# The opening and the first three staged blocks of a decoder trunk, written as one pipeline with every engine's order fixed

## The chip, the cores and the metric

The kernel runs on one core of one Trainium2 chip. A core has a matrix engine (TensorE, "PE" in the profile, whose weight loads have a row of their own, "PEld"), VectorE ("DVE"), ScalarE ("ACT"), GpSimd ("POOL"), a queue engine ("SP") and 16 DMA engines, which all queues share. The metric is device time in microseconds, the median of several executions.

## The reference

A two-layer causal decoder trunk on 256 tokens of width 2048, all in float32. Every sub-layer is modulated by vectors worked out from a conditioning vector `c`:

```python
cond = silu(c)
for l in range(2):
    sh1, sc1, g1, sh2, sc2, g2 = split(cond @ ada_w[l] + ada_b[l], 6)   # ada_w[l]: 2048 x 12288
    h = rmsnorm(x, norm_mix_g[l]) * (1 + sc1) + sh1
    y = mixer_ab(h, ...) if l == 0 else mixer_c(h, ...)
    x = x + g1 * y
    h = rmsnorm(x, norm_ffn_g[l]) * (1 + sc2) + sh2
    x = x + g2 * ((silu(h @ w1) * (h @ w3)) @ w2)
return rmsnorm(x, final_g)
```

`mixer_ab` begins with one projection `h @ ab_w_in` (2048 x 4096). Its first half becomes a gated causal convolution of width 31, its second half a chunked causal gate with a layer norm and a 128 x 128 spatial weight per head. The part of the kernel that the change touches is everything from the first load to the first three 512-wide column groups of that projection.

## The kernel before, in words

The 256 tokens are two blocks `b` of 128 on the partitions. A weight is read in loads of 512 KB (`load`, L182: 256 rows by 512 columns; `load_wide`, L191: 128 rows by 1024 columns), all issued on SP and all into one ring of 12 buffers (`RAW`). For products in nearly float32 precision each load is split (L163) into a rounded `hi`, cast by ACT (L167), and a rest `lo`, subtracted by DVE (L168). The activations are split in the same way (`ah`, `al`). Each pair of 128 x 128 tiles then takes three matmuls: hi by ah, hi by al (L216, L217) and lo by ah (L222). The load's buffer is free again after the DVE subtraction. A `unit` (L198) is two loads, two splits and 24 matmuls for one quarter (512 rows) of the inner dimension and one group of 512 output columns.

The modulation vectors come from `mod_cols` (L368), a generator that works out 512 of the 2048 columns of one vector in four steps, each with two loads of `ada_w`. A scale runs on PE with the conditioning vector as the weights (L381), into a PSUM bank `ps_ada` of which there is one. A shift, except in the first quarter, runs on DVE as a weighted sum `accq` (L386, L388). At the end `put_cols` (L403) turns the row into columns: eight small PE instructions (L408) into the one-bank pool `msp`, then additions on DVE (L414, or L417 and L418).

`norm_cols` (L436) makes such a pair of generators, scale and shift, for each quarter of the inner dimension. `started` (L539) uses them in a staged way: the projection's quarter `q` can run as soon as quarter `q` of scale and shift is known. Block `q` first scales the normalised, transposed tokens (`scaled`, L492; h on ACT and DVE at L500 and L502, then the splits at L489 and L490), then runs three units, the third into two banks named `mt`. Between the halves of its units (`between`, L531) it advances the two generators of quarter `q + 1`, so that a block holds 6 weight loads and 16 adaLN loads, the last one only 6.

Before these blocks comes an opening: `consts` (L70) loads `c`, gathers six small tables by DMAs on ACT's queue into one tile `stage`, transposes it (L113), and does the same for the adaLN bias `st_b` (L121 to L124). `run` (L967) loads `x`, and takes its sums of squares on ACT (`sumsq`, L454). `mixer_ab` (L605) issues four larger tables on ACT's queue: the spatial weights (`b_w_s`, 512 KB), the convolution weights (`a_conv_w`, 31 rows, 124 KB) and two norm vectors. `entry` work (`start`, `prep`) normalises the tokens and transposes them (L477, L480, L518). `params` (L627) transposes the spatial and the convolution weights through `msp` (L636, L637, L641, L642) and spreads the two norm vectors over the partitions (`to_bcast`, L423: L432 to L434). It is called after block 0.

The order of the instructions on each engine is not that of the text. A planner sorts each engine's instructions ahead of time by priority, which is the place in the text, and by when it expects operands and buffers to be there; it may bring a later instruction forward. On the chip each engine then runs its list strictly in order. Tiles with the same tag share a fixed number of slots. The tag "t" has three, for `cs`, `stage`, `st_b`, the normalised rows `xr`, and `rhi` and `rlo` of `to_bcast`.

## Time and profile before

| | us |
|---|---|
| median of 3 runs | 2014.65 |
| lowest and highest | 2011.18 and 2015.0 |
| the profiled execution, its own time | 2018.89 |
| its span | 2017.2 |
| PE busy within the span | 1957.5 |
| DVE busy | 1420.8 |
| ACT busy | 840.2 |
| mean HBM traffic | 267 GB/s |

The profile is one execution. Its page gives each engine's busy time, the chain of work that ended last, the costliest groups of instructions (line of the code, engine, operation, result <- operands, shape, count, busy us, mean ns of one, idle time before them and what ended it), and the DMA issues. The trace behind it can be asked for stretches of time: a row then has the busy time of PE, PEld, DVE, ACT and POOL with counts, the granted clock of PE as a share of full speed, the busy share of the DMA engines and GB/s. In the order of time, a row has start, duration, engine, line, and in brackets the idle time before it with what ended that. "SPq" is the issue of a DMA by SP, not its transfer.

### The profile page before, as it was taken

The page shows a single profiled execution, that of the slowest core. Times are in us where ns is not written, and L with a number is a line of the kernel's source. Part 1 is how long each engine was busy: PE and PEld are TensorE (multiplying, and loading weights), DVE is VectorE, ACT ScalarE, POOL GpSimd, SP SyncE. Part 2 cuts the span into 40 slices and gives each one's busy share as a digit, 9 for nine tenths or more (in the row PEclk, how much of TensorE's full clock was granted, in tenths as well). Part 3 has the DMA queues.
Part 4 walks back from the last instruction along what each step waited for, and adds up shares of the span by engine and source line. Part 5 has one row for each costly group of instructions (what it writes and reads, how often), then busy time and mean ns, then how long its engine had stood idle before and what let it go on. Part 6 is the DMA issues. An engine that isn't in the chain of part 4 may idle for free.

```text
span 2017.2 us, 24298 instructions
## 1 busy us (share of the span) xinstructions
PE 1957.5 (97%) x8896; PEld 1542.4 (76%) x8896; DVE 1420.8 (70%) x1709; ACT 840.2 (42%) x1023; POOL 34.2 (2%) x91
## 2 busy tenths in 40 slices
PE   5989999998999999999999999999999999999998
PEld 2567677777887888887878887788788888888886
DVE  2667999788778888777887788867555444554455
ACT  3234343454444334443344347544433444334443
POOL 0000000000000000000120000000000000000000
PEclk9889999989999999999999999999999999999999
DMA  9998988879888899888988887889656666566651
GB/s 329 351 369 266 339 277 284 270 252 343 294 277 327 316 341 331 300 295 316 343 308 292 289 286 264 324 276 326 198 187 191 189 189 191 183 189 190 193 184 48
DMA packets 250344, 540.39 MB, mean 268 GB/s; under 512 B 16521, under 2 KB 17849, under 8 KB 249840
## 3 DMA queue, kind: packets, MB, share of 16 engines
q1 hardware_dynamic: 248472, 536.99, 78.2%
q10 hardware_dynamic: 1752, 1.86, 0.3%
q8 instruction: 69, 1.13, 0.2%
q14 instruction: 51, 0.42, 0.1%
HBM read 536.68 MB, written 2.10 MB: 267 GB/s over the span
## 4 chain that ended last, share of the span: by engine, by line
PE 95%; DVE 2%; DMA 2%; ACT 1%; issue 0%; POOL 0%; ACTq 0%; POOLq 0%; DVEq 0%
PE mm L216 28%; PE mm L217 27%; PE mm L222 27%; PE ps_ada L381 3%; PE ps_col L408 2%; PE mt L216 1%; PE mt L217 1%; PE tp L591 1%; PE mt L222 1%; DVE accq L388 1%; PE ps_ada L315 1%; PE tp L480 1%; DMA st_b<-in_ada_b_dram 1%; PE tp L838 1%; DMA raw<-in_pool_w_dram 0%
## 5 line engine op out<-in xcount | busy, mean ns | idle before, releaser
L167 ACT CAST hi<-raw 128x1024 fp32r<-128x1024 f32 x632 | 665.1, 1053 | 986.1 <-PE mm L217 898.2
L168 DVE TENSOR_TENSOR lo<-raw,hi 128x1024 fp32r<-128x1024 f32 x632 | 771.1, 1223 | 423.6 <-ACT hi L167 413.3
L216 PE MATMUL mm<-hi,ah 128*128 128x512 f32 x1568 | 619.5, 396 | 6.0 <-ACT hi L167 3.4
L217 PE MATMUL mm<-hi,al 128*128 128x512 f32 x1568 | 613.6, 392 | 0.0
L222 PE MATMUL mm<-lo,ah 128*128 128x512 f32 x1568 | 422.9, 390 | 0.0
L216 PEld LDWEIGHTS mm<-hi,ah 128*128 128x128 f32 x1568 | 296.0, 189 | 94.3 <-ACT hi L167 14.4
L217 PEld LDWEIGHTS mm<-hi,al 128*128 128x128 f32 x1568 | 296.1, 189 | 62.9 <-DVE accq L388 1.7
L222 PEld LDWEIGHTS mm<-lo,ah 128*128 128x128 f32 x1568 | 295.6, 189 | 61.7
L216 PE MATMUL mm<-hi,hh 128*128 128x512 f32 x704 | 279.9, 398 | 0.0
L217 PE MATMUL mm<-hi,hl 128*128 128x512 f32 x704 | 277.4, 394 | 0.0
L353 DVE SCALAR_TENSOR_TENSOR acc<-raw,cond,acc 128x1024 f32<-128x1024 f32 x180 | 230.6, 1281 | 5.3 <-DMA raw<-in_ada_w_dram 3.7
L222 PE MATMUL mm<-lo,hh 128*128 128x512 f32 x704 | 194.7, 395 | 0.0
L216 PEld LDWEIGHTS mm<-hi,hh 128*128 128x128 f32 x704 | 132.1, 188 | 34.7 <-ACT hi L167 1.7
L222 PEld LDWEIGHTS mm<-lo,hh 128*128 128x128 f32 x704 | 132.1, 188 | 32.1
L217 PEld LDWEIGHTS mm<-hi,hl 128*128 128x128 f32 x704 | 132.1, 188 | 30.8
L388 DVE SCALAR_TENSOR_TENSOR accq<-raw,cond,accq 128x512 f32<-128x512 f32 x135 | 101.1, 749 | 4.8 <-DMA raw<-in_ada_w_dram 2.1
L676 DVE SCALAR_TENSOR_TENSOR co<-aT,cw,co 128x256 f32<-128x256 f32 x240 | 99.5, 479 | 0.0
L216 PE MATMUL mm<-hi,mh 128*128 128x512 f32 x160 | 64.8, 406 | 1.6 <-ACT mh L489 1.6
L599 DVE TENSOR_TENSOR gy<-mm,gate 128x512 f32<-128x512 f32 x72 | 47.1, 686 | 24.3 <-PE mm L222 23.9
L217 PE MATMUL mm<-hi,ml 128*128 128x512 f32 x160 | 63.8, 401 | 0.3 <-DVE ml L490 0.3
L381 PE MATMUL ps_ada<-raw,cond 128*32 128x512 f32 x352 | 62.3, 629 | 0.0
L600 DVE TENSOR_TENSOR x<-x,gy 128x512 f32<-128x512 f32 x72 | 47.2, 688 | 0.1
(169 smaller groups left out, 990.6 us busy)
## 6 DMA issues: line engine op xcount, KB each, us to landing
raw<-in_ffn_w_dram SPq DMA_DIRECT2D x528, 512.0 KB, 4.8
raw<-in_ada_w_dram SPq DMA_DIRECT2D x384, 512.0 KB, 5.7
raw<-in_ab_w_in_dram SPq DMA_DIRECT2D x64, 512.0 KB, 6.5
raw<-in_ab_w_out_dram SPq DMA_DIRECT2D x32, 512.0 KB, 5.7
raw<-in_pool_w_dram SPq DMA_DIRECT2D x8, 512.0 KB
x<-in_x_dram SPq DMA_DIRECT2D x2, 1024.0 KB, 6.5
gate<-in_final_g_dram SPq DMA_DIRECT2D x1, 1024.0 KB
out_dram<-x SPq DMA_DIRECT2D x2, 512.0 KB
```

The source lines that it names most:

```text
L167: nc.scalar.copy(hi, raw)
L168: nc.vector.tensor_tensor(lo, raw, hi.bitcast(F32), op=ALU.subtract)
L216: nc.tensor.matmul(ps[b], act[b][0][:, kk, :], hi[:, k, :], start=first and kk == 0, stop=False)
L217: nc.tensor.matmul(ps[b], act[b][1][:, kk, :], hi[:, k, :], start=False, stop=False)
L222: self.nc.tensor.matmul(ps[b], act[b][0][:, kk, :], lo[:, k, :], start=False, stop=last and kk == 3)
L353: nc.vector.scalar_tensor_tensor(acc, raw, self.cond[:, k : k + 1], acc, op0=ALU.mult, op1=ALU.add)
L381: nc.tensor.matmul(acc[32 * j : 32 * j + 32, :], self.cond[:, k : k + 1].to_broadcast([P, 32]), raws[j // 2][:, j % 2, :], start=u == 0, s ...
L388: nc.vector.scalar_tensor_tensor(acc, raws[j // 2][:, j % 2, :], self.cond[:, k : k + 1], acc, op0=ALU.mult, op1=ALU.add)
L408: nc.tensor.matmul(ps[:, a : a + 1], src[:, P * a : P * a + P], one, start=u == 0, stop=u == len(parts) - 1,)
L599: nc.vector.tensor_tensor(t, ps, g[:, 512 * q : 512 * q + 512], op=ALU.mult)
L600: nc.vector.tensor_tensor(xs, xs, t, op=ALU.add)
L676: nc.vector.scalar_tensor_tensor(co[:, k, :], src, cw[:, k, j : j + 1], co[:, k, :], op0=ALU.mult, op1=ALU.add,)
```

## The change

The opening moves out of `consts` and `run` into a new function `opening`, whose text is a pipeline: steps of the first quarter's scale (`next(sc)`) and shift (`next(sh)`) stand between the loads of `x`, the small tables and the entry work of the two token blocks. All the small loads go on SP's queue instead of ACT's, `stage` gets a place of its own and its memset goes to POOL. The four larger tables become a function `tables`, also on SP, called after block 0; `params` is called after block 1 instead of block 0.

In `started` both loads of a unit are split before its products, and the generators advance after each half. With `staged=True` a generator of quarters 1 to 3 yields after its fourth step and not before `put_cols`, so the row copy and the column products come in the middle of the third unit. A new context manager `in_order` ties each instruction on PE, DVE, ACT and SP that is traced within it to the one before it on the same engine, which adds no wait on the chip but takes from the planner the freedom to reorder. It is put around the opening and the four blocks of the first layer's projection. `started` is also used by the first layer's channel mixer, there without the fixed order.

```diff
...
 AF = mybir.ActivationFunctionType
 ALU = mybir.AluOpType
 PSUM = bass.MemoryType.PSUM
+ENG = mybir.EngineType
+ORDERED = (ENG.PE, ENG.DVE, ENG.Activation, ENG.SP)
+AFTER = mybir.DependencyInfo(mybir.DependencyClass.NoSync, mybir.DependencyReason.DATA)
 
 P = 128
 D = 2048
...
     def consts(self):
         nc, c = self.nc, self.cpool
         i = self.i
-        cs = self.wk.tile([KT, P], F32, name="cs", tag="t", bufs=3)
-        nc.sync.dma_start(out=cs, in_=i["c"].rearrange("a (k p) -> (a k) p", p=P))
         warm = c.tile([P, 1], F32, name="warm")
         nc.vector.memset(warm, 0.0)
         nc.scalar.activation(warm, warm, AF.Silu)
...
         for j in range(4):
             nc.gpsimd.memset(self.pick[32 * j : 32 * j + 1, :], 1.0)
 
+    def opening(self, e):
+
+        nc, c, i = self.nc, self.cpool, self.i
+        sc, sh = e.parts[0]
+        cs = self.wk.tile([KT, P], F32, name="cs", tag="t", bufs=3)
+        nc.sync.dma_start(out=cs, in_=i["c"].rearrange("a (k p) -> (a k) p", p=P))
         ps = self.msp.tile([P, 512], F32, name="ps_c", tag="ms")
         nc.tensor.transpose(ps[:, :KT], cs, self.ident[:KT, :KT])
         self.cond = c.tile([P, KT], F32, name="cond")
         nc.scalar.activation(self.cond, ps[:, :KT], AF.Silu)
-        stage = self.wk.tile([P, P], F32, name="stage", tag="t", bufs=3)
-        nc.vector.memset(stage, 0.0)
+
+        def tokens(b):
+            nc.sync.dma_start(out=self.x[b], in_=i["x"][0, b * P : (b + 1) * P, :])
+            for q in range(4):
+                self.sumsq(b, q)
+
+        def entry(b):
+            e.start(b)
+            for q in range(4):
+                e.prep(b, q)
+
+        stage = c.tile([P, P], F32, name="stage")
+        nc.gpsimd.memset(stage, 0.0)
         rows = {}
         r = 0
 
         def put(name, ap, n):
             nonlocal r
-            nc.scalar.dma_start(out=stage[r : r + n, :], in_=ap)
+            nc.sync.dma_start(out=stage[r : r + n, :], in_=ap)
             rows[name] = r
             r += n
 
+        next(sc)
+        next(sc)
+        tokens(0)
+        next(sc)
         put("mix_g", i["norm_mix_g"].rearrange("l (k p) -> (l k) p", p=P), 2 * KT)
+        tokens(1)
+        entry(0)
+        next(sc)
         put("ffn_g", i["norm_ffn_g"].rearrange("l (k p) -> (l k) p", p=P), 2 * KT)
+        st = [self.wk.tile([P, P], F32, name=f"st_b{l}", tag="t", bufs=3) for l in range(2)]
+        for l in range(2):
+            nc.sync.dma_start(out=st[l][: 6 * KT, :], in_=i["ada_b"][l].rearrange("(k p) -> k p", p=P))
+        next(sh)
         put("conv_b", i["a_conv_b"].rearrange("l (k p) -> (l k) p", p=P), HT)
         put("a_g", i["a_norm_g"].rearrange("l (k p) -> (l k) p", p=P), HT)
         put("a_b", i["a_norm_b"].rearrange("l (k p) -> (l k) p", p=P), HT)
         put("b_bias", i["b_bias"].rearrange("l h t -> (l h) t"), HT)
+        next(sh)
+        self.adab = c.tile([P, 2, 6 * KT], F32, name="adab")
+        for l in range(2):
+            ps = self.msp.tile([P, 512], F32, name="ps_b", tag="ms")
+            nc.tensor.transpose(ps[:, : 6 * KT], st[l][: 6 * KT, :], self.ident[: 6 * KT, : 6 * KT])
+            nc.vector.tensor_copy(self.adab[:, l, :], ps[:, : 6 * KT])
+        entry(1)
         ps = self.msp.tile([P, 512], F32, name="ps_c", tag="ms")
         nc.tensor.transpose(ps[:, :P], stage, self.ident)
         cols = c.tile([P, P], F32, name="cols")
         nc.vector.tensor_copy(cols, ps[:, :P])
         self.col = lambda name, k: cols[:, rows[name] + k : rows[name] + k + 1]
         self.cols = lambda name, k, n: cols[:, rows[name] + k : rows[name] + k + n]
-        self.adab = c.tile([P, 2, 6 * KT], F32, name="adab")
-        for l in range(2):
-            st = self.wk.tile([P, P], F32, name="st_b", tag="t", bufs=3)
-            nc.scalar.dma_start(out=st[: 6 * KT, :], in_=i["ada_b"][l].rearrange("(k p) -> k p", p=P))
-            ps = self.msp.tile([P, 512], F32, name="ps_b", tag="ms")
-            nc.tensor.transpose(ps[:, : 6 * KT], st[: 6 * KT, :], self.ident[: 6 * KT, : 6 * KT])
-            nc.vector.tensor_copy(self.adab[:, l, :], ps[:, : 6 * KT])
+        self.close(sc)
+        next(sh)
+        next(sh)
+        self.close(sh)
 
     def bands(self, tiles):
 
...
             self.put_cols([(acc, self.ones[:, :1])], HT, l, v, HT * hh, dst, gname)
             yield
 
-    def mod_cols(self, l, v, q, on_pe, dst, gname=None):
+    def mod_cols(self, l, v, q, on_pe, dst, gname=None, staged=False):
 
 
         nc = self.nc
...
                     nc.vector.scalar_tensor_tensor(
                         acc, raws[j // 2][:, j % 2, :], self.cond[:, k : k + 1], acc, op0=ALU.mult, op1=ALU.add
                     )
-            if u < 3:
+            if u < 3 or staged:
                 yield
         if on_pe:
             rows = self.wk.tile([P, 512], F32, name="rows", tag="rows", bufs=1)
...
             parts = [(rows, self.pick)]
         else:
             parts = [(acc, self.ones[:, :1])]
-        yield
+        if not staged:
+            yield
         self.put_cols(parts, 4, l, v, 4 * q, dst, gname)
         yield
 
...
     def norm_cols(self, e, l, sc, sh, gname):
 
         e.parts = [
-            self.add(self.mod_cols(l, sc, q, True, e.gs, gname), self.mod_cols(l, sh, q, q == 0, e.sh))
+            self.add(
+                self.mod_cols(l, sc, q, True, e.gs, gname, staged=q > 0),
+                self.mod_cols(l, sh, q, q == 0, e.sh, staged=q > 0),
+            )
             for q in range(4)
         ]
 
...
             elif slot == 4:
                 self.close(g)
 
-    def started(self, e, w_cols, rate, then=None):
+    @contextmanager
+    def in_order(self):
+
+        traced = self.nc.cur_bb.bb.instructions
+        n = len(traced)
+        yield
+        before = {}
+        for ins in traced[n:]:
+            if ins.engine in ORDERED:
+                if ins.engine in before:
+                    self.tc.add_manual_dep(ins, before[ins.engine].name, AFTER, reason="in_order")
+                before[ins.engine] = ins
+
+    def started(self, e, w_cols, rate, then={}):
 
 
 
...
             e.act[q] = [self.scaled(e.act[q][b], q, b, e.gs, e.sh) for b in range(NB)]
             nxt = e.parts[q + 1] if q < 3 else ()
             for u, (w, col0) in enumerate(w_cols):
-                self.unit(
-                    w, 512 * q, col0, e.act[q], ps[u], q == 0, q == 3, lambda: self.between(nxt, 2 * u)
-                )
-                self.between(nxt, 2 * u + 1)
-            if q == 0 and then is not None:
-                then()
+                raws = [self.load(w, 512 * q + 256 * h, col0) for h in range(2)]
+                cuts = [self.split(raw) for raw in raws]
+                for h, (hi, lo) in enumerate(cuts):
+                    for b in range(NB):
+                        self.products(hi, lo, h, e.act[q], b, ps[u], q == 0)
+                    for b in range(NB):
+                        self.products_lo(hi, lo, h, e.act[q], b, ps[u], q == 3)
+                    self.between(nxt, 2 * u + h)
+                self.after_unit()
+            if q in then:
+                then[q]()
         self.rate = rate
         return ps
 
...
             cwr = raw[:, 2:, :].rearrange("p a n -> p (a n)")
             nrm = p.tile([P, 2, 512], F32, name="nrm", tag="co")
             nc.gpsimd.memset(nrm, 0.0)
-            nc.scalar.dma_start(out=ws, in_=i["b_w_s"][0].rearrange("h t s -> t h s"))
-            nc.scalar.dma_start(out=cwr[:CW, :], in_=i["a_conv_w"][0])
-            for n, name in enumerate(("b_norm_g", "b_norm_b")):
-                nc.scalar.dma_start(out=nrm[0:64:32, n, :], in_=i[name][0].rearrange("(j n) -> j n", n=512))
+
+            def tables():
+                nc.sync.dma_start(out=ws, in_=i["b_w_s"][0].rearrange("h t s -> t h s"))
+                nc.sync.dma_start(out=cwr[:CW, :], in_=i["a_conv_w"][0])
+                for n, name in enumerate(("b_norm_g", "b_norm_b")):
+                    nc.sync.dma_start(out=nrm[0:64:32, n, :], in_=i[name][0].rearrange("(j n) -> j n", n=512))
 
             def params():
 
...
                 self.to_bcast(nrm[:, 0, :], bg, 2)
                 self.to_bcast(nrm[:, 1, :], bb, 2)
 
-            for b in range(NB):
-                e.start(b)
-                for q in range(4):
-                    e.prep(b, q)
-            held = self.started(e, [(w_in, 0), (w_in, DH), (w_in, 512)], RATES[0], params)
+            with self.in_order():
+                self.opening(e)
+                held = self.started(
+                    e, [(w_in, 0), (w_in, DH), (w_in, 512)], RATES[0], {0: tables, 1: params}
+                )
             act = e.act
 
             co = p.tile([P, HT, T], F32, name="co", tag="co")
...
         nc, i = self.nc, self.i
         self.ss = [None] * NB
         self.consts()
-        self.x = []
-        for b in range(NB):
-            xb = self.xpool.tile([P, D], F32, name=f"x{b}")
-            nc.sync.dma_start(out=xb, in_=i["x"][0, b * P : (b + 1) * P, :])
-            self.x.append(xb)
-            for q in range(4):
-                self.sumsq(b, q)
+        self.x = [self.xpool.tile([P, D], F32, name=f"x{b}") for b in range(NB)]
 
         def cols(name):
             return self.cpool.tile([P, KT], F32, name=name)
...
         last = Entry(self, None, None, None)
 
         self.norm_cols(mix0, 0, SC1, SH1, "mix_g")
-        self.finish(mix0.parts[0][:1])
         self.g1 = self.gate()
         self.gen_g1 = self.add(self.bcast(0, G1, True, self.g1))
         scale = [self.mod_cols(0, SC2, q, True, ffn0.gs, "ffn_g") for q in range(4)]
...
```

More of the change, by code (lines that the diff above doesn't have):

```diff
@@ L1 @@
-from contextlib import ExitStack
+from contextlib import ExitStack, contextmanager
 import concourse.bass as bass
```

## The prediction

> **What bounds the kernel now.** I read the page first, then busy time by stretches, then the instructions in order of time, because the page's averages mix stages with different limits.
>
> ```profile
> span 2017.2 us, 24298 instructions
> PE 1957.5 (97%) x8896; PEld 1542.4 (76%) x8896; DVE 1420.8 (70%) x1709; ACT 840.2 (42%) x1023; POOL 34.2 (2%) x91
> 2.40:23.00 20.60, 5.10 (x15) 1.39 (x16) 1.54 (x7) 5.65 (x17) 2.80 (x4) 1.00 0.84 286
> 23.00:85.00 62.00, 52.21 (x250) 29.81 (x244) 32.74 (x56) 21.05 (x35) 0.55 (x1) 0.86 1.05 387
> 85.00:100.00 15.00, 15.00 (x66) 7.69 (x65) 11.34 (x15) 4.24 (x6) 0.00 (x0) 1.00 0.84 272
> 115.00:130.00 15.00, 15.00 (x75) 9.62 (x74) 13.82 (x18) 3.66 (x5) 0.00 (x0) 1.00 0.96 322
> 160.00:165.00 5.00, 5.00 (x24) 4.14 (x23) 3.29 (x5) 3.27 (x5) 0.00 (x0) 1.00 0.52 146
> 200.00:250.00 50.00, 50.00 (x252) 33.18 (x250) 47.13 (x93) 15.32 (x18) 0.00 (x0) 1.00 0.95 339
> ```
>
> A stretch's row gives PE, PEld, DVE, ACT and POOL busy, then granted clock, DMA share and GB/s. Over the whole span PE is the bound (97%). The changed part, up to the end of the staged projections, is different: from 23 to 85 us the DMA engines are full (1.05) at 387 GB/s while PE is busy 52 of 62 us. There the loads bind, and 387 GB/s is my rate. They fall short in the opening (286), from 85 to 100 (272) and from 115 to 130 (322): 5.4 + 4.5 + 2.5 = 12 us of transfer. At 160 it is the other way round: PE is full and the loads wait.
>
> ```profile
> 45.89 0.80 PE L216 MATMUL mm<-hi,ah 128*128 128x512 f32 x1 [3.39 <-ACT hi L167]
> 53.82 0.50 PE L216 MATMUL mm<-hi,ah 128*128 128x512 f32 x1
> 119.34 1.07 PE L222 MATMUL mm<-lo,ah 128*128 128x512 f32 x4
> 123.28 1.07 PE L222 MATMUL mm<-lo,ah 128*128 128x512 f32 x4
> 138.57 1.84 PE L408 MATMUL ps_col<-ones,accq 128*128 128x1 f32 x8 [3.57 <-DVE accq L388]
> 149.47 1.07 PE L222 MATMUL mm<-lo,ah 128*128 128x512 f32 x4
> 152.19 1.07 PE L222 MATMUL mm<-lo,ah 128*128 128x512 f32 x4
> 163.07 1.07 PE L222 MATMUL mt<-lo,ah 128*128 128x512 f32 x4
> ```
>
> These rows give the units. Half a unit (12 matmuls) takes 152.19 - 149.47 = 2.72 us; with one scale step behind it, 123.28 - 119.34 = 3.94; the first such pair after PE has idled, 53.82 - 45.89 = 7.93. The staged blocks end at 163.07 + 1.07 = **164.1 us**. From 200 to 250 PE has no idle time left, so I price the change as the shift of this point and let the rest follow it unchanged.
>
> **The change: where the loads go.** All small tables move from ACT's queue to SP's, among the weight loads; the x loads come after four adaLN loads; the sumsq work still waits for x on ACT. The spatial-weight and convolution tables are issued after the first block.
>
> ```profile
> 2.00:3.00 1.00, 0.26 (x1) 0.18 (x1) 0.00 (x0) 0.81 (x2) 0.94 (x2) 1.00 0.44 92
> 2.12 0.96 POOL L621 MEMSET nrm<- 128x1024 f32 x1
> 18.00:19.00 1.00, 0.00 (x0) 0.00 (x0) 0.00 (x0) 0.00 (x0) 0.00 (x0) 1.00 0.38 135
> 20.00:21.00 1.00, 0.13 (x1) 0.16 (x1) 0.00 (x0) 0.00 (x0) 0.00 (x0) 1.00 0.07 24
> SPq L185 <- DMA prm<-in_a_conv_w_dram: 7.0, 1, 7.0
> raw<-in_ada_w_dram SPq DMA_DIRECT2D x384, 512.0 KB, 5.7
> prm<-in_a_conv_w_dram ACTq DMA_DIRECT2D x1, 124.0 KB
> L123 PE MATMUL ps_b<-ident,st_b 96*128 96x96 f32 x2 | 0.8, 407 | 6.6 <-DMA st_b<-in_ada_b_dram 6.2 <-DVE cols L115 0.4
> ```
>
> In the opening of before, SP's next load waited 7.0 us for the convolution table, and PE 6.2 us for the adaLN bias. At 20 us the whole core moves 24 GB/s, a sixteenth of 387: one DMA engine of sixteen is still sending. I read this as the 31-row table (124 KB) lying on one engine: 127 KB at 24 GB/s is 5.3 us, where an even spread takes 0.3. [...] After the change the table stands in SP's own queue; every later load has a share behind it on that engine, so the loads of blocks 1 to 3 come 4.8 us later (bounds 0 and 5.0, the difference from an even spread; I take 4.8, near the upper, since the 24 GB/s row measures it; with an even spread the end below would be 160.3). The wait of the opening goes; its price moves to block 1.
>
> PE's own opening gets longer in text order: the copies of the first transposed x tiles stand on ACT behind the second x tile's sums, and block 0's first product would start near 41 us instead of 45.9. It hides: block 0's third unit waits for its load at about 59 us anyway.
>
> Time of the load that decides block 1, the third unit's first: 59 loads of 0.524 MB lead up to and include it (16 + 22 + 21), plus x 2.10, tables 0.66 and rows 0.15, together 33.85 MB. At 387 GB/s that is 87.5 us; with 2.4 us before the stream starts (the row at 2.00 has 92 GB/s), 4.8 for the one-engine table and 0.8 for landing and for the small descriptors (an estimate between 0 and the 4 us of rival C) it lands at **95.5 us**.
>
> Two waits are new on SP: its first small row waits for the `stage` memset, now on POOL behind the memset that ends at 3.1 us, and by then SP has six loads and x ahead of it, so it costs nothing; ACT loses its DMA issues and idles there anyway.
>
> **The handoffs.** The new generators yield after their fourth step, so the column products (L408) come in the middle of the third unit, between two halves of products, in place of an idle PE. Before, that gap was 3.57 us at 138.57, and two like it. This is a real gain for PE, but in blocks 0 and 1 the loads bind, so it pays nothing there. The added order holds up nothing I can see inside a block: DVE's 16 weighted sums and six lo splits fit into the 30 us that 22 loads take.
>
> **The parameters.** `params` moves from after block 0, where its instructions were strewn among products, to after block 1, and is now fixed as a solid piece: nothing of block 2 on PE, DVE or ACT may pass it.
>
> ```profile
> L636 PE MATMUL tp<-ident,prm 128*128 128x128 f32 x8 | 1.7, 350 | 0.3 <-DVE sh L414 0.3
> L637 DVE COPY wcT<-tp 128x512 f32<-128x512 f32 x2 | 1.4, 688 | 1.0 <-PE tp L636 1.0
> L641 PE MATMUL tp<-ident,prm 31*128 31x31 f32 x8 | 0.9, 226 | 0.0
> L642 DVE COPY cw<-tp 128x124 f32<-128x124 f32 x2 | 0.6, 289 | 2.2 <-PE tp L641 2.2
> L433 PE MATMUL ps_bc<-rlo,identr 128*128 128x512 f32 x4 | 1.6, 394 | 0.0
> L434 ACT COPY bgb<-ps_bc 128x512 f32<-128x512 f32 x4 | 2.4, 588 | 12.0 <-PE ps_bc L433 12.0
> L489 ACT CAST rhi<-nrm 128x512 fp32r<-128x512 f32 x2 | 1.3, 626 | 0.0
> L490 DVE TENSOR_TENSOR rlo<-nrm,rhi 128x512 fp32r<-128x512 f32 x2 | 1.4, 691 | 1.8 <-ACT rhi L489 1.1 <-PE ps_bc L432 0.7
> L500 ACT ACTIVATE h<-xT,sh,gs 128x128 f32<-128x128 f32 x16 | 7.0, 485 | 16.6 <-DVE sh L414 16.6
> L489 ACT CAST ah<-h 128x512 fp32r<-128x512 f32 x8 | 4.9, 612 | 0.0
> L167 ACT CAST hi<-raw 128x1024 fp32r<-128x1024 f32 x28 | 28.9, 1045 | 18.8 <-DMA raw<-in_ab_w_in_dram 10.9 <-PE mm L217 4.9 <-DMA raw<-in_ada_w_dram 1.7
> L408 PE MATMUL ps_col<-pick,rows 128*128 128x1 f32 x40 | 5.2, 252 | 3.7 <-ACT rows L395 3.7
> ```
>
> It is serial, since each result goes through the one `msp` bank (0.05 us per hand-over). Twice four transposes 0.6, copy 0.69, four short ones 0.4, copy 0.29: 4.4. First broadcast: rlo 0.69 and second product 0.4, copy 0.59, then a pair 0.62 and its copy 0.59: 3.1. The second also waits for its rhi: 3.8. Sum **11.3 us**. Behind it on ACT stand block 2's own preparations, four h at 0.44, two ah at 0.61, a hi cast 1.05: 4.1 more before the first product. All the while no raw buffer of block 2 is freed; the twelve hold 16 us of loads, less what was already waiting, and then SP stops.
>
> **The sum.** Block 1's third unit: cast 1.05, half 2.72, the two column products with their adds 2.45 (L408: 5.2 / 5 = 1.04 each), half 2.72, so it ends at 95.5 + 8.9 = 104.4. Parameters and preparations: 104.4 + 15.4 = 119.8. Block 2 on a PE that idled: 7.93 + 3 x 3.94 + 2.72 + 2.45 + 4.1 = 29.0, so block 3 starts at 148.8. Its loads are there: 6 x 2.72 = 16.3. End: **165.1 us** against 164.1, a loss of 1.0. The profiled execution took 2018.89 us, 1.7 more than its span of 2017.2; it would take 2019.9. It lies 0.2% above the median, so I add 1.0 to the median of the three runs, 2014.65: **2015.7**. About 10 us gained in the opening and at the handoffs are given back by the parameter piece.
>
> **The rivals.**
> A, faster: the buffers cover the parameter piece and the loads stay the bound to the end. Then block 2's third unit's first load lands at 2.4 + 45.4 MB / 387 GB/s + 4.8 + 0.8 = 125.3, block 3 starts at 125.3 + 1.05 + 2.72 + 2.45 + 4.1 = 135.6 and ends at 151.9: minus 12.2, **2002.4**. For it: within a block PE needs 4 x 3.94 + 2 x 2.72 + 2.45 = 23.7 us of the 29.8 that 22 loads take. Against it: 15.4 us is near all that twelve buffers hold, and block 2 alone needs 29 of PE.
>
> B, slower: the clock falls in block 1. There PE waits for loads twice for 2 x 1.35 (shift pair) + 1.35 + 1.05 - 1.0 = 4.1 us, and the rows at 45.89 and 138.57 show PE slow after idling 3.4 and 3.6 us (a column group 1.84 against 1.04). A cold third unit: 12 x 0.2 for the half, 0.8 for the column group, 1.0 in the second half: plus 4.2, in all 5.2, **2019.9**. [...]
>
> C, slower: in the opening the bias tiles share three slots with the x rows. If SP must wait for transposes behind the second x tile, SP stands still until about 21 us with all loads landed by 19: about 4 us with the latency, plus 5.0 in all: **2019.7**. If the bias takes its slots first, nothing.
>
> D: the fixed order equals what the planner already did; no change, 2014.6.
>
> **How the numbers follow.** Forecast (2015.7, within plus or minus 4) 0.38; A 0.22; B 0.20; C 0.14; D 0.06. About 0.2%, 4 us, is what a measurement can tell from no change. So faster 0.23, same 0.43, slower 0.34. The range goes from A's 2003 to 2023, which takes in C with half of B.
>
> **What would show it.** First product near 41 us; no stretch under 350 GB/s from 5 to 60 us; one DMA-engine tail just after block 0; a PE hole of about 15 us between blocks 1 and 2 near 104 us with the DMA rate falling inside it; staged end near 165. The forecast is wrong if the hole is short or filled, if DMA runs through it, or if 300 us onward shifts for reasons of its own.

## The result and the profile after

| | before | after |
|---|---|---|
| median of the timed runs, us | 2014.83 | 2035.51 |
| lowest and highest | 2011.18, 2017.73 | 2033.56, 2037.42 |
| ratio after to before, 95% interval | | 1.0104, 1.0084 to 1.0123 |
| span of the profiled execution | 2017.2 | 2035.7 |
| start of the staged blocks' last product of lo | 163.8 | 183.4 |

The change costs 20.7 us. The profiled executions lie 4.1 and 1.9 us above these medians, so their spans differ by 18.5. The staged blocks end 19.6 us later, and from there to the end the two need the same time to 1.1 us (1853.4 and 1852.3). So the loss lies where the change is. The page of after, its span and PE's row:

```profile
span 2035.7 us, 24287 instructions
PE 1965.6 (97%) x8896; PEld 1545.6 (76%) x8896; DVE 1422.3 (70%) x1708; ACT 841.4 (41%) x1023; POOL 34.8 (2%) x92
```

PE does the same 8896 instructions, in 8.1 us more: some of them run at a lower clock (0.50 from 40 to 50 and from 130 to 140, below). The rest of the loss is idle time. Busy time by stretches of after (PE, PEld, DVE, ACT, POOL, granted clock, DMA share, GB/s):

```profile
10.00:20.00 10.00, 4.07 (x20) 1.14 (x16) 2.04 (x6) 5.08 (x15) 0.55 (x1) 0.97 0.93 359
20.00:30.00 10.00, 7.00 (x26) 2.22 (x28) 0.00 (x0) 3.41 (x7) 0.00 (x0) 0.51 0.61 199
30.00:40.00 10.00, 6.64 (x31) 3.94 (x31) 2.75 (x9) 2.24 (x4) 0.55 (x1) 0.83 1.02 378
40.00:50.00 10.00, 6.53 (x30) 3.38 (x29) 1.98 (x8) 2.86 (x6) 0.00 (x0) 0.50 1.05 386
50.00:60.00 10.00, 7.98 (x28) 5.38 (x29) 8.76 (x13) 4.51 (x5) 0.00 (x0) 0.65 0.79 266
...
120.00:130.00 10.00, 5.22 (x18) 2.50 (x18) 3.74 (x8) 2.17 (x4) 0.00 (x0) 0.76 0.17 63
130.00:140.00 10.00, 4.85 (x11) 3.39 (x12) 5.48 (x9) 7.26 (x12) 0.00 (x0) 0.50 0.12 31
```

Three stretches stand out. From 20 to 30 the loads fall to 199 GB/s and PE's clock to 0.51. From 50 to 60 they fall again, to 266. From 120 to 140 they nearly stop (63 and 31) while PE is busy half the time. What SP, ACT, DVE and PE do there, in order of time (start, duration, engine, line, operation, idle time before). Line numbers are those of the changed kernel: L218 is a load, L200 and L201 are the cast and the subtraction of its split, L249 and L255 the products of hi and of lo by ah, L135 the load of a bias tile:

```profile
9.79 0.33 SPq L120 DMA_DIRECT2D stage<-in_norm_ffn_g_dram  x1
18.04 0.33 SPq L135 DMA_DIRECT2D st_b<-in_ada_b_dram  x1
18.47 0.66 SPq L192 DMA_DIRECT2D brow<-in_ada_b_dram  x1
22.37 0.33 SPq L135 DMA_DIRECT2D st_b<-in_ada_b_dram  x1
...
44.69 0.88 SPq L218 DMA_DIRECT2D raw<-in_ab_w_in_dram  x2
53.25 2.69 SPq L218 DMA_DIRECT2D raw<-in_ada_w_dram  x3
...
114.25 1.77 SPq L218 DMA_DIRECT2D raw<-in_ab_w_in_dram  x2
137.60 2.69 SPq L218 DMA_DIRECT2D raw<-in_ada_w_dram  x3
```

```profile
52.00 2.36 DVE L201 TENSOR_TENSOR lo<-raw,hi 128x1024 fp32r<-128x1024 f32 x2 [0.26 <-ACT hi L200]
...
71.11 1.04 ACT L200 CAST hi<-raw 128x1024 fp32r<-128x1024 f32 x1 [16.01 <-DMA raw<-in_ab_w_in_dram]
...
108.86 1.04 ACT L200 CAST hi<-raw 128x1024 fp32r<-128x1024 f32 x1 [10.87 <-DMA raw<-in_ab_w_in_dram]
```

```profile
21.23 1.97 PE L517 MATMUL tp<-ident,xr 128*128 128x128 f32 x8 [3.21 <-ACT xT L555]
...
41.02 3.64 PE L414 MATMUL ps_ada<-raw,cond 128*32 128x512 f32 x16
45.45 1.86 PE L442 MATMUL ps_col<-pick,rows 128*128 128x1 f32 x8 [0.79 <-ACT rows L428]
52.02 0.79 PE L249 MATMUL mm<-hi,ah 128*128 128x512 f32 x1 [4.71 <-ACT hi L200]
...
109.96 0.50 PE L249 MATMUL mt<-hi,ah 128*128 128x512 f32 x1 [3.31 <-ACT hi L200]
...
114.93 0.68 PE L249 MATMUL mt<-hi,ah 128*128 128x512 f32 x1
115.40 0.63 PE L250 MATMUL mt<-hi,al 128*128 128x512 f32 x1
...
119.34 0.60 PE L693 MATMUL tp<-ident,prm 128*128 128x128 f32 x4
...
130.75 0.63 PE L467 MATMUL ps_bc<-rlo,identr 128*128 128x512 f32 x1
136.37 0.80 PE L249 MATMUL mm<-hi,ah 128*128 128x512 f32 x1 [4.99 <-ACT hi L200]
```

SP's own waits (what it waited for, us in total, times, longest):

```profile
SPq L135 <- DVE xr L514: 7.1, 1, 7.1
...
SPq L218 <- DMA prm<-in_a_conv_w_dram: 5.0, 1, 5.0
...
SPq L135 <- PE tp L517: 3.9, 2, 3.1
```

SP cannot pass a bias tile until a slot is free. It stands 7.9 us ahead of the first (10.1 to 18.0, 7.1 of them for the row scaling) and 3.2 ahead of the second (19.1 to 22.4, for the transposes), and issues no load of a weight from 8.8 to 22.7. It stops again from 45.6 to 53.3, with all twelve buffers full. In the fixed order ACT casts block 0's first load only behind the preparation of block 0's `h` and `ah`; the cast ends at 52.0, and with its result start both block 0's first product (52.02) and the DVE subtraction that frees the first buffer at 53.2. In what follows the first product stands for this moment. SP stops a third time from 116.0 to 137.6, while PE, ACT and DVE work through the parameters one after the other: 17.0 us pass from the first transpose of the parameters (119.34) to the first product of block 2 (136.37). ACT's casts at 71.11 and 108.86 are those of the third units of blocks 0 and 1, and both wait for their load.

### The profile page after: what moved, and what is told of

It is laid out like the page before. It is cut to its first block, busy times and chain, and to the rows that moved or that the text cites. A ratio compares the mean times of both kernels' runs of the same rounds, so it can differ in the third digit from the quotient of the medians.

```text
span 2035.7 us, 24287 instructions
## 1 busy us (share of the span) xinstructions
PE 1965.6 (97%) x8896; PEld 1545.6 (76%) x8896; DVE 1422.3 (70%) x1708; ACT 841.4 (41%) x1023; POOL 34.8 (2%) x92
## 3 DMA queue, kind: packets, MB, share of 16 engines
q10 hardware_dynamic: 288, 1.05, 0.1%
## 4 chain that ended last, share of the span: by engine, by line
PE 89%; DVE 2%; issue 0%; ACT 0%; DMA 0%; POOL 0%; POOLq 0%; DVEq 0%; ACTq 0%
PE mm L249 27%; PE mm L250 27%; PE mm L255 27%; PE ps_ada L414 1%; PE tp L646 1%; PE ps_col L442 1%; PE ps_ada L348 1%; PE mt L249 1%; PE mt L250 1%; PE mt L255 1%; PE tp L895 1%; DVE accq L421 0%; PE tp L517 0%; DVE lo L201 0%; PE ps_ada L364 0%
## 5 line engine op out<-in xcount | busy, mean ns | idle before, releaser
L200 ACT CAST hi<-raw 128x1024 fp32r<-128x1024 f32 x632 | 665.0, 1054 | 1037.1 <-PE mm L250 909.1
L201 DVE TENSOR_TENSOR lo<-raw,hi 128x1024 fp32r<-128x1024 f32 x632 | 770.9, 1223 | 424.2 <-ACT hi L200 414.8
L249 PE MATMUL mm<-hi,ah 128*128 128x512 f32 x1568 | 622.4, 397 | 19.3 <-ACT hi L200 16.7
L255 PE MATMUL mm<-lo,ah 128*128 128x512 f32 x1568 | 424.8, 392 | 0.0
L249 PEld LDWEIGHTS mm<-hi,ah 128*128 128x128 f32 x1568 | 297.2, 190 | 109.9 <-ACT hi L200 28.5
L255 PEld LDWEIGHTS mm<-lo,ah 128*128 128x128 f32 x1568 | 297.3, 190 | 62.3
L249 PE MATMUL mm<-hi,hh 128*128 128x512 f32 x704 | 279.9, 398 | 0.0
L255 PE MATMUL mm<-lo,hh 128*128 128x512 f32 x704 | 194.8, 395 | 0.0
L249 PEld LDWEIGHTS mm<-hi,hh 128*128 128x128 f32 x704 | 132.2, 188 | 34.4 <-ACT hi L200 1.7
L255 PEld LDWEIGHTS mm<-lo,hh 128*128 128x128 f32 x704 | 132.2, 188 | 32.0
L249 PE MATMUL mm<-hi,mh 128*128 128x512 f32 x160 | 64.5, 404 | 1.6 <-ACT mh L526 1.6
```

The source lines that it names most:

```text
L200: nc.scalar.copy(hi, raw)
L201: nc.vector.tensor_tensor(lo, raw, hi.bitcast(F32), op=ALU.subtract)
L249: nc.tensor.matmul(ps[b], act[b][0][:, kk, :], hi[:, k, :], start=first and kk == 0, stop=False)
L255: self.nc.tensor.matmul(ps[b], act[b][0][:, kk, :], lo[:, k, :], start=False, stop=last and kk == 3)
```

## The experiments

Theory 1: the solid parameter piece stops the loads of block 2 and makes the hole. Theory 2: the opening costs as well, through the bias tiles' slots, through PE's clock, or both. Theory 3, from the prediction: the 31-row table lies on one DMA engine and delays every load behind it. The rivals of each are in the expectations. Every run was compared with the kernel before, timed beside it (medians 2016.27, 2016.11 and 2017.03 in the three sets).

The table puts all versions in one frame. The columns are read from the instructions in order of time: the start of block 0's first product, the start of the cast of block 1's third unit, the last product of lo in `mt` (start), the span, and the differences between them. "Warm" versions have 50 transposes added in the opening; "three, cold" is all four edits without these transposes. PE is called cold where its granted clock is 0.50. Each row is one profiled execution.

| version | first product | cast, block 1 unit 3 | between | last lo | from the cast | span | behind |
|---|---|---|---|---|---|---|---|
| after | 52.02 | 108.86 | 56.8 | 183.4 | 74.5 | 2035.7 | 1852.3 |
| bias own | 48.28 | 104.50 | 56.2 | 179.1 | 74.6 | 2035.2 | 1856.1 |
| params loose | 47.33 | 103.08 | 55.8 | 164.2 | 61.1 | 2016.9 | 1852.7 |
| both of these | 48.25 | 105.36 | 57.1 | 165.6 | 60.2 | 2018.3 | 1852.7 |
| even table | 47.79 | 98.50 | 50.7 | 173.5 | 75.0 | 2029.7 | 1856.2 |
| params last | 51.78 | 107.95 | 56.2 | 166.2 | 58.3 | 2023.4 | 1857.2 |
| warm, bias own | 42.07 | 98.61 | 56.5 | 174.5 | 75.9 | 2023.8 | 1849.3 |
| warm only | 46.97 | 102.81 | 55.8 | 177.5 | 74.7 | 2026.8 | 1849.3 |
| all four | 42.09 | 93.79 | 51.7 | 153.9 | 60.1 | 2006.7 | 1852.8 |
| three, cold | 48.36 | 99.97 | 51.6 | 160.2 | 60.2 | 2008.4 | 1848.2 |

**The bias tiles in a buffer of their own.**

```diff
-        st = [self.wk.tile([P, P], F32, name=f"st_b{l}", tag="t", bufs=3) for l in range(2)]
+        sb = self.accp.tile([P, 2, P], F32, name="st_b", tag="acc")
+        st = [sb[:, l, :] for l in range(2)]
```

> The changed kernel with one edit: the two adaLN bias tiles take the free accumulator slot instead of two of the three shared work slots. Theory 1 (two serial places: SP stands still behind the bias tiles in the opening, and the parameter piece between blocks 1 and 2): SP no longer waits for the row scaling and the transposes (7.1 and 3.9 us in the changed kernel), the first product of block 0 comes at 42 to 46 us instead of 52.0, the third unit's load of block 0 is cast near 61 instead of 71.1, and the staged end moves from 183.8 to about 174: 2025 to 2028 us. Rival 2 (the fixed order as such costs, everywhere a little): SP's wait goes but the staged end moves by under 3 us: 2033 to 2036. Rival 3 (the one-engine table decides): 2033 to 2036.

Measured 2034.97 (ratio 1.009, 1.0059 to 1.012): a miss. Three of the four executions took 2033.4 to 2036.9 us and one 2024.88; the profile is that of the slowest. The standstill at 20 is gone; the stretch below has 370 GB/s where after moves 51 from 20 to 25. But the first product comes only at 48.28, and SP stands with full buffers from 41.8 to 49.5 instead. The last lo is 4.3 us earlier, and 3.8 of that are lost again behind the staged blocks.

```profile
20.00:25.00 5.00, 3.84 (x16) 1.77 (x16) 0.00 (x0) 2.68 (x7) 0.00 (x0) 0.50 1.03 370
45.00:50.00 5.00, 1.72 (x4) 1.43 (x5) 3.64 (x6) 4.45 (x7) 0.00 (x0) 0.50 0.41 152
```

So the slots alone are not what makes the first product late: the stop is moved, not removed.

**The parameters out of the fixed order**, at the same place in the text.

```diff
-        for ins in traced[n:]:
-            if ins.engine in ORDERED:
+        for k, ins in enumerate(traced[n:], n):
+            if ins.engine in ORDERED and k not in self.loose:
```

> The changed kernel with one edit: the instructions of the parameter function are left out of the fixed order, so the planner may strew them among products again. Theory 1: the hole of 17 us between blocks 1 and 2 (119.3 to 136.4) shrinks to under 5 us, DMA runs on inside it, and the staged end comes 10 to 16 us earlier: 2019 to 2026 us. Rival 2: the hole is made of waits that the order makes elsewhere too, staged end moves by under 4 us: 2031 to 2036. Rival 3: 2033 to 2036.

Measured 2018.49 (1.0015, 1.0003 to 1.0027), 0.5 us below the expected range; the staged end moves by 19.2 us, more than the 10 to 16 expected. The last lo starts at 164.2:

```profile
L255 PE MATMUL mt<-lo,ah x24: 388/389/432, 111.9 to 183.4; 128*128 128x512 f32 x24
```

```profile
L255 PE MATMUL mt<-lo,ah x24: 388/393/632, 107.8 to 164.2; 128*128 128x512 f32 x24
```

The first row is that of after, the second that of this version (count, least, median and longest duration in ns, first and last start). 13.4 of the 19.2 us lie between the cast and the last lo (74.5 against 61.1). The other 5.8 lie ahead of the parameters, 4.7 of them in the first product, in an opening whose PE order is the same: there the clock was higher in this execution (0.66 from 20 to 25 against 0.50).

**Both edits** (the two diffs above).

> Both edits together on the changed kernel (bias tiles in the accumulator slot, parameters outside the fixed order). Theory 1: the two add up, staged end at 158 to 165 us against 164.1 of the kernel before the change: 2009 to 2017 us. Rival 2: at most 6 us together, 2028 or more. Rival 3: 2030 or more.

Measured 2019.89 (1.0021, 1.0005 to 1.0036): a miss, the gains do not add. In the table the first product is at 48.25, no earlier than with either edit alone: something else holds the opening there. The 4.3 us of the bias edit and the 13.4 of the parameters would put the last lo at 165.7, and it is at 165.6; what does not add is the earlier opening that the version with the parameters loose had.

**The new text with nothing pinned.**

```diff
-            if ins.engine in ORDERED:
+            if ins.engine in ():
```

> The changed kernel without the fixed order: the new text, but the planner is free to sort as before. Theory 1: the parameters are strewn again, and the bias tiles may or may not be brought forward by the planner: 2015 to 2026 us. Rival 2: the whole loss goes, 2010 to 2016. Rival 3 (the one-engine table, which the text moves): 2030 to 2036, since the table's place stays.

Measured 2012.71 (0.9993, 0.9981 to 1.0005), below theory 1's range and within rival 2's: the whole loss goes with the fixed order, and the text by itself costs nothing. The planner starts block 0 at 41.69 and strews the parameters; the last lo is at 165.8. It also brings back the gap of 3.57 us before the shift's column products that the pinned order had removed.

**The table as 16 and 15 rows**, a direct test of theory 3.

```diff
-                nc.sync.dma_start(out=cwr[:CW, :], in_=i["a_conv_w"][0])
+                nc.sync.dma_start(out=cwr[:16, :], in_=i["a_conv_w"][0][:16])
+                nc.sync.dma_start(out=cwr[16:CW, :], in_=i["a_conv_w"][0][16:])
```

> The changed kernel with the convolution table sent as 16 and 15 rows in place of 31. Theory (one DMA engine carries the 31 rows, and its share of every later load stands behind them): the 4.8 us of that engine go, so block 1's third unit casts its first load about 4.8 us earlier than at 108.9, near 104, block 1 ends near 114.5, and the staged blocks end near 179 with the hole of the parameters unchanged at 17; the total, by what the earlier bias tiles gave (4.3 us of the staged end, 0.5 of the total), 2031 to 2035. Rival (the twelve full buffers, not that engine, set when block 1's loads land): the cast stays within 1.5 us of 108.9 and the staged end near 183.8, the time 2034 to 2037.

Measured 2030.23 (1.0078, 1.0056 to 1.01). The stretches from 70 to 90, first of after, then of this version:

```profile
70.00:80.00 10.00, 7.70 (x39) 6.36 (x36) 5.67 (x11) 4.86 (x8) 1.69 (x1) 0.87 1.03 332
80.00:90.00 10.00, 8.96 (x40) 5.72 (x41) 6.17 (x9) 2.72 (x3) 0.00 (x0) 0.95 0.91 330
```

```profile
70.00:80.00 10.00, 9.36 (x39) 7.28 (x38) 4.49 (x12) 4.80 (x8) 1.04 (x1) 0.75 1.04 380
80.00:90.00 10.00, 10.00 (x56) 5.82 (x54) 8.89 (x11) 2.11 (x2) 0.00 (x0) 1.00 1.05 387
```

The cast moves by 10.4 us, but 4.2 of that is an earlier first product, again with a higher clock in the opening (0.69 against 0.51 from 20 to 30). The column "between" takes that out: 50.7 to 51.7 with the even table, 55.8 to 57.1 without. Theory 3 holds. The pair that differs in the table alone and has the same first product to 0.1 us is "both of these" and "three, cold": the cast comes at 105.36 and at 99.97, the last lo at 165.6 and at 160.2, 5.4 us earlier in both places. SP's wait for the landing of the table (5.0 us in after) is gone with the even table. The total is 0.8 us below the expected range.

**The parameters behind the last staged block**, still pinned.

```diff
-                    e, [(w_in, 0), (w_in, DH), (w_in, 512)], RATES[0], {0: tables, 1: params}
+                    e, [(w_in, 0), (w_in, DH), (w_in, 512)], RATES[0], {0: tables, 3: params}
```

> The changed kernel with the parameters' solid piece behind the last staged block in place of behind block 1; still in the fixed order. Theory (the piece costs because it is solid: nothing behind it on PE, DVE and ACT may pass, wherever it stands): the hole of 17 us between blocks 1 and 2 goes, the staged blocks end at 183.8 - 17 = 167, and a stop of PE of 10 to 12 us with the same chain comes right behind, of which only the 4 us of block 2's preparations are saved: 2026 to 2033. Rival (it costs because it stands in front of blocks that live from hand to mouth: it stops the stream of loads; behind the staged blocks the work of the next part fills it): no hole over 4 us at the staged end, 2015 to 2022.

Measured 2022.93 (1.0031, 1.0017 to 1.0045), 0.9 us above the rival's range and 3.1 below the theory's. The hole is gone and none comes behind:

```profile
165.50 1.07 PE L255 MATMUL mt<-lo,ah 128*128 128x512 f32 x4
166.41 0.60 PE L693 MATMUL tp<-ident,prm 128*128 128x128 f32 x4
166.76 0.48 PE L249 MATMUL mm<-hi,ah 128*128 128x512 f32 x1
```

The products behind the staged blocks are outside the fixed order, so they fill the piece: PE is busy without a break from 155 to 195. The part behind the staged blocks is 4.9 us longer than in after, but that column spreads by 9 us over the versions, so this is no price of the parameters. What costs between blocks 1 and 2 is not the parameter work, it is that nothing may pass it.

**Added work for PE in the opening.** 50 transposes of the unit matrix, results unused, with the bias tiles in their own buffer.

```diff
+        def warm(n):
+            for _ in range(n):
+                nc.tensor.transpose(idle[:, :P], self.ident, self.ident)
...
+            if b:
+                warm(10)
             for q in range(4):
                 e.prep(b, q)
+                if (b, q) == (0, 1):
+                    warm(16)
...
         self.close(sh)
+        warm(24)
```

> The bias tiles' own buffer, and 50 transposes of the unit matrix added to PE's fixed order in the opening, 16 between the first x tile's transposes, 10 before the second's, 24 before the first product; their results are not used. Theory (with the loads no longer stopped, the clock sets the opening: PE's granted clock is 0.50 to 0.58 from 20 to 30 and 35 to 50, and the serial chain through PE takes 5 us more for it): the clock in 35 to 45 is over 0.9, the first product comes 3 to 5 us earlier than at 48.3, near 44, the third unit of block 1 casts near 100.5 in place of 104.5, the staged blocks end near 175. Rival (the chain waits on ACT, DVE and POOL, and PE's clock only shows it): the first product stays between 47 and 50 and the staged end near 179. In the total 2030 to 2035 either way.

Measured 2025.84 (1.0059, 1.004 to 1.0079). PE's rows and three stretches of this version:

```profile
18.02 1.95 PE L112 MATMUL idle<-ident 128*128 128x128 f32 x16
20.54 1.14 PE L529 MATMUL tp<-ident,xr 128*128 128x128 f32 x8 [0.56 <-ACT xT L567]
...
33.60 1.92 PE L426 MATMUL ps_ada<-raw,cond 128*32 128x512 f32 x16
36.31 1.05 PE L454 MATMUL ps_col<-pick,rows 128*128 128x1 f32 x8 [0.79 <-ACT rows L440]
37.22 2.82 PE L112 MATMUL idle<-ident 128*128 128x128 f32 x24
42.07 0.50 PE L261 MATMUL mm<-hi,ah 128*128 128x512 f32 x1 [2.03 <-ACT hi L212]
```

```profile
20.00:30.00 10.00, 7.25 (x47) 3.10 (x48) 1.63 (x7) 2.63 (x6) 0.55 (x1) 1.00 1.04 381
30.00:40.00 10.00, 8.59 (x72) 6.32 (x70) 3.05 (x10) 5.02 (x10) 0.00 (x0) 1.00 1.05 386
40.00:50.00 10.00, 7.97 (x42) 4.72 (x41) 8.76 (x13) 4.62 (x5) 0.00 (x0) 1.00 1.05 387
```

The same sixteen `ps_ada` matmuls take 1.92 us instead of 3.64, the same eight column products 1.05 instead of 1.86. The clock is 1.00, the first product comes 6.2 us earlier than with the bias edit alone, and the buffers never fill: 387 GB/s from 40 to 50. The cast is 5.9 us earlier, the last lo 4.6. The total is 4.2 us below the expected range: behind the last lo this execution takes 1849.3 us and that of the bias edit 1856.1, and why was not followed.

**The added transposes alone** (the diff above, without the buffer).

> The changed kernel with the 50 added transposes and nothing else: the bias tiles still wait for the shared slots, the parameters are still solid. Theory (the two delays of the opening are in series up to the second x tile, and behind that only the clock counts): first product at 45 to 47.5 in place of 52.0, block 1's third unit casts its first load 56 to 57 us behind it, at 101.5 to 104, the last product of lo at 176 to 178 in place of 183.4, 2028 to 2032. Rival (the standstill of the loads at 20 us alone makes the first product late): first product over 50, 2034 to 2037.

Measured 2031.95 (1.0072, 1.0056 to 1.0088), as expected: first product 46.97, though the clock falls to 0.50 again from 25 to 30 (0.73 over 20 to 30). Counted from after's 52.02, the transposes alone bring it forward by 5.05 us, the slots alone by 3.74, and both together by 9.95, 1.2 more than the sum. These two single shares do not stand firm: four versions with the same opening have 47.33, 47.79, 51.78 and 52.02, and counted from 47.33 the transposes alone are worth 0.4 us and the slots alone nothing. Firm is the price of the transposes once the bias tiles have their buffer: 48.25, 48.28 and 48.36 without them, 42.07 and 42.09 with them, 6.2 us.

**All four edits** (buffer, loose parameters, even table, transposes), and then the same without the transposes.

> All four edits at once: the bias tiles' own buffer, the table as 16 and 15 rows, the parameters out of the fixed order, the 50 added transposes. If the four prices add: from the version with the first and third (staged end 166.0, 2019.9) minus 4.8 for the table and minus 4 for the clock, a staged end near 157 and 2009 to 2013, below the kernel before. If they do not add, because block 2's third unit or PE itself is the bound by then: a staged end of 162 to 166 and 2013 to 2020.

Measured 2006.57, faster than the kernel before: 0.9957, 0.9942 to 0.9972. It is 2.4 us below the expected range. The last lo is at 153.9, 3 us earlier than the sum of the four prices said, so the four edits together give no less than the sum.

> The version with all four edits, without its 50 added transposes. Theory (the added transposes keep PE's clock up in the opening, and the first product's lateness passes through the twelve full buffers into block 1's loads one for one): first product at 47 to 48.5 in place of 42.1, block 1's third unit casts its first load 51 to 52 us behind the first product, at 98.5 to 100, the staged blocks' last product of lo at 158 to 160 in place of 153.9, and 2009 to 2014 in place of 2006.6. Rival (the opening hides and the loads alone set block 1): the cast within 1.5 of 93.8, the same time to 2 us.

Measured 2012.14 (0.9983, 0.9968 to 0.9998). First product and cast are where the theory put them (48.36, 99.97), the last lo 0.2 us behind its range (160.2). Without the transposes the three come 6.3, 6.2 and 6.3 us later: the lateness of the opening goes one for one into the end of the staged blocks.

**The even table in the unpinned text and in the kernel before.** The first is the unpinned version with the even table and the bias tiles' own buffer.

> The rewritten text with no engine pinned, the bias tiles in their own buffer and the convolution table as 16 and 15 rows; no added transposes. Theory (the even table is worth about 5 us of load time to any version whose blocks are bound by loads): the staged blocks' last product of lo at 159 to 162 in place of the 165.8 of the text alone, 2006 to 2011 in place of 2012.7. Rival (without the pinning the staged blocks are bound by PE): within 2 us of 2012.7.

Measured 2007.39 (0.9955, 0.9938 to 0.9971), as fast as the pinned version with all four edits, without added work. Its first product is at 39.70, its last lo at 158.5, slightly earlier than expected. Since two edits were made, the 7.3 us against the text alone are not the table's by themselves.

```diff
-            nc.scalar.dma_start(out=cwr[:CW, :], in_=i["a_conv_w"][0])
+            nc.scalar.dma_start(out=cwr[:16, :], in_=i["a_conv_w"][0][:16])
+            nc.scalar.dma_start(out=cwr[16:CW, :], in_=i["a_conv_w"][0][16:])
```

> The kernel before with its convolution table as 16 and 15 rows. Theory (one DMA engine carries the 31 rows; in the opening of before SP's next load waited 7.0 us for that landing and the core moved 24 GB/s at 20): the stop goes, the stream of loads runs through 15 to 25, block 1's loads come about 5 us earlier, the last product of lo at 158 to 160 in place of 163.8, 2009 to 2012. Rival (the opening's chain through the adaLN bias and PE covers it): first product within 1 us of 45.9 and 2014 to 2017.

Measured 2013.06 (0.9982, 0.9971 to 0.9994), 1 us above the range; the positions are as expected, the first product at 41.34 and the last lo at 159.3, each 4.5 us earlier than before. SP's waits of the first 30 us:

```profile
SPq L185 <- DMA raw<-in_ada_w_dram: 8.8, 11, 1.7
SPq L185 <- DMA stage<-in_norm_mix_g_dram: 5.7, 1, 5.7
SPq L185 <- DMA x<-in_x_dram: 2.2, 1, 2.2
```

The 7.0 us for the convolution table are gone from the list. In the position of the last lo the table cost the kernel before 4.5 us, nearly the 5.4 that it costs the changed one.

## Why the prediction was wrong

The forecast was 2015.7 with a range to 2023; measured are 2035.5. The forecast end of the staged blocks, 165.1, compares with 183.4 + 0.4 = 183.8. The 18.7 us between them, term by term:

| step of the prediction | forecast | after | off by |
|---|---|---|---|
| cast of block 1's third unit | 95.5 | 108.86 | 13.4 |
| from there to the end of block 1 | 8.9 | 10.5 | 1.6 |
| parameters and preparations | 15.4 | 17.0 | 1.6 |
| block 2 | 29.0 | 29.2 | 0.2 |
| block 3 | 16.3 | 18.2 | 1.9 |

**The failed step is "It hides".** The prediction put block 0's first product near 41 us, and said a later one would do no harm, because block 0's third unit waits for its load at about 59 us anyway. Both halves fell. The prediction shows no working for its 41, and with the clock at 1.00 and the slots out of the way it is right to 1.1 us (42.07). In after the opening runs at a clock of 0.50 to 0.51 from 20 to 30 and from 40 to 50, and the first product comes at 52.0. And it does not hide. Until block 0's first load is cast no buffer comes free and SP stands, so the load that was to land at 59 is issued only at 63.28, and the third unit's cast comes at 71.1. Of the 13.4 us, 10.3 are this (108.86 against 98.61 once both are mended). The remaining 3.1 are put down to the load sum: the mended versions have it too, and it was not taken apart further.

**Rival B was real, and wider than it was priced.** It priced a cold third unit in block 1 at 5.2 us. In after the first half of that unit stays warm behind a wait of 3.31 us (clock 1.00 from 109.96 to 114.93; the second unit is cold behind one of 4.15, 0.54 from 94 to 101), but the second half, from 114.93 on, has products of 0.63 us in place of 0.39 and takes 4.41 us in place of 2.72, at a mean clock of 0.61. That is the 1.6 us by which block 1 ends late. The first half of block 3 is cold in the same way (165.54 to 169.99, mean clock 0.62), which is most of the 1.9 us there. The largest part is in the opening, which is cold for most of 30 us: 6.2 us, the price of the transposes with the bias tiles in their own buffer.

**Rival C's stop was real too**: SP issues no load of a weight from 8.8 to 22.7. What it cost by itself stays open. Its 4 us agree with 3.74 for the first product and 4.3 for the last lo, counted from after, but two versions with the shared slots and a higher clock have the first product at 47.33 and 47.79, earlier than the 48.28 with the slots out of the way. It had a chance of 0.14 and was priced as if it were alone; B and C came together, on one chain.

**The one-engine table was right in kind and nearly in size**: 4.8 us forecast, with an upper bound of 5.0, and 5.4 measured. That the table lies on one engine is an inference from before's stretch from 20 to 21, where the DMA share is 0.07, a sixteenth of the 1.05 of the full stretches. With 16 and 15 rows SP's waits for the table are gone, 7.0 us in before and 5.0 in after. But the kernel before pays nearly the same (4.5), so the table explains at most 1 us of the difference between the two kernels.

**The parameter hole was right in place and kind**, and 1.6 us short. The sum had the serial chain at warm durations; in the hole PE runs at 0.50 (130 to 140). What was wrong was its weight. The prediction expected an early end of block 1 to pay for it ("about 10 us gained in the opening and at the handoffs are given back by the parameter piece"). The opening lost instead (first product 52.0 against 45.9 before), so the piece is a loss on its own: 13.4 to 15.8 us, from the column "from the cast" (74.5 to 75.9 with it, 60.1 to 61.1 without).

**The handoffs** behave as said: in after the column products stand between two halves of products and the 3.57 us gap is gone. That it pays nothing in the load-bound blocks 0 and 1 was not tested apart.

**The shift of one point** as a measure of the total holds to about 7 us: the time behind the last lo is 1853.4 before and runs from 1846.2 (text only) to 1857.2 (parameters last). Why it varies was followed only for the bias edit: of its 3.8 us, 2.3 are lost between two POOL instructions that stand at 383 and 447 in it, where the stretch from 380 to 390 has a clock of 0.66 in that version and 1.00 in after. A different phase of later work is likely behind it; that was not tested.

What stays open is why the same PE order of the opening gives a first product at 47.3 to 47.8 in two versions and at 51.8 to 52.0 in two others. The profiles show that the clock differs and where (in after it first falls at 19.5, with parameters loose at 14.0), not what makes it differ.

## What to carry to other kernels

Pinning an order fixes its waits too: before pinning a stretch, look in it for a serial chain through one small buffer, and leave that chain free or put it where unpinned work can fill it (here 13.4 to 15.8 us). A late first consumer (here the cast of the first load) does not hide behind loads that are themselves waiting for its buffers; follow the ring to the last buffer before writing "it hides" (here 6.3 us at the first product came to 6.3 at the last lo). And price a sparse opening at both clocks, since the same sixteen `ps_ada` matmuls took 1.92 us at a clock of 1.00 and 3.64 at 0.50.

## What was not expected of the hardware

The granted clock stays low though PE has work. In after it is 0.50 from 40 to 50 with PE busy 6.53 of 10 us and no gap over 0.8 us between 41.0 and 47.3; in the version with added transposes and the bias buffer the same chain runs from 30 to 40, at 1.00 with 8.59 of 10 us busy. The length of a gap does not decide it alone. In after the clock is 1.00 up to 19.25 and 0.50 from 19.50 on, 1.5 us into the gap of 3.21 us before 21.23; with the parameters loose, in the same opening, it falls at 14.0 (mean 0.90 from 10 to 15), when PE has been at work again for 1.0 us behind a gap of 2.10. And behind the longer gap of 3.31 us before 109.96 the products take 0.39 us, at a clock of 1.00.

The changes of the clock in after, up to 116 us, lie at whole multiples of 3.41 us from one another. By its mean over steps of 0.1 us, it falls at 19.46, rises at 29.70, falls at 36.53, rises at 57.01, falls at 77.49, rises at 80.90, falls at 94.56, rises at 101.38 and falls at 115.04: 10.24, 6.83, 20.48, 20.48, 3.41, 13.66, 6.82 and 13.66 us. The fall at 14.0 with the parameters loose lies 5.5 us ahead of that at 19.46, which is no such multiple, so the places of the changes differ between these two executions. That would fit the different clocks of equal openings; that it is their cause was not shown.

A table of 124 KB in 31 rows, 0.02% of the 540 MB that the kernel moves, is worth 4.5 us of the staged blocks to the kernel before and 5.4 us to the changed one.
